# Hybrid decoder block on one core: a constant tile for the norm's eps, and where the pool of split operands begins

## The chip, the cores and the metric

The kernel runs on one core of one Trainium2 chip. The metric is the device time of one execution in microseconds (us). Before the change the median of three runs is 1487.4 us (1486.57 to 1491.19).

## What is computed

One decoder block for 1024 tokens of width 1024, float32 throughout. The reference, cut down:

```python
proj = x @ w_in                      # 1024 x 7168: q, f, i, og, pool_v, gate_a, gate_b
q = silu(q) * 128 ** -0.5;  f = lb + (1 - lb) * sigmoid(f);  k = 1 - f
o = hgrn2_chunked(q, k, i, log(f))   # 8 heads of 128: S_t = diag(f_t) S_{t-1} + k_t v_t^T, o_t = S_t^T q_t
o = o * rsqrt(mean(o ** 2, axis=-1) + RMS_EPS)          # the norm of the change, RMS_EPS = 1e-6
a = (o * hgrn_norm_g * sigmoid(og)) @ w_a
b = grouped(causal_mean(pool_v) - pool_v) @ w_pool * pool_scale
mix = (sigmoid(gate_a) * a + sigmoid(gate_b) * b) @ w_out
x = layer_norm(2 ** 0.25 * x + mix)
x = layer_norm(2 ** 0.25 * x + relu(x @ w_up) ** 2 @ w_down)
```

## The kernel before

**Products.** TensorE multiplies a stationary operand (up to 128 x 128) by a moving one (128 x up to 512) into PSUM. To keep float32's precision, each large product is made of three matmuls in the type fp32r: an operand is split into a high part (a cast on ScalarE) and a low part (a subtraction on VectorE), and high x high, high x low and low x high are added up in PSUM. Lines 108 to 110 (`mm3`), 202 to 205 (`prod`), 478 to 480 (`three`) and 1295 to 1297 (`down_tile`) are these three matmuls. In the profile a matmul is written with its moving operand first: `ps_pj<-act,w` moves an `act` tile past a stationary `w` tile. On top of that, the large products are Strassen products: seven instead of eight half-size ones (`p1` to `p7` in `pair`, line 264 on), with sums and differences of operands made on VectorE.

**Stages, in order of time.** First i = the value projection, by rows (`three`, to about 75 us). Then the eight heads, each in two halves of 512 tokens (`hgrn`, lines 819 to 946): the recurrence of a half is made of small plain float32 matmuls, many VectorE operations and a chain on GpSimd, while TensorE runs the projections of the next head, of the gates and of the pooling branch between them (`prod`, to about 600 us). Then the pool products (`pool_products`, line 709, by `mm3`), the product with w_a (`prod`), the product with w_out and the first layer norm (`mix`, `mm3`, from about 765 us), the up-projection (`prod`, to about 1160 us) and the down-projection (`down_tile`, to the end).

**Memory.** A core's on-chip memory is 128 partitions; a tile takes the same bytes in each, rounded up to 32. Pools on the left are laid one behind the other from byte 16512 on, pools on the right downward from the top. On the left stand, in this order, `const` (ident, cmask, eps_ln, inv_n, prm, lb, one_lb, e01), `stat` (eight tiles of 48 bytes allotted 64, four of 16 allotted 32), then `act`: 28 tiles of 4096 bytes, each the high and the low half of a split activation (later of anything that is split). Behind it stand `ca` (intermediate results) and, in turn, the heads' pool `hgp`, the rows of the first norm and the weights of the down-projection. On the right, under a pad of 24 floats (line 78), stand `wq` (the split weights `w`, raw weights, differences `t`) and, in turn, x, the heads' `q`, `f`, `og`, `v`, the split w_out rows `wo`, and buffers of the MLP. Which pool a tile is in is fixed in the code; the addresses follow from the sizes and the order.

**Order of the work.** A scheduler with a timeline of its own orders each engine's instructions, so the order can shift when an instruction's form changes.

**Lines the text speaks of.** 121 and 122: the split of a weight into `w`; 126 and 127: the split into `act`; 163: transposes; 242: a difference of raw weights; 595: loads. In `hgrn`: 824 the scan, 832 to 851 the small factors on GpSimd, 883 and 943 transposes, 888, 928, 931 the small products, 936 the squares and their sums (ScalarE), 940 the scaling by the root. Between 936 and 940 stands `inverse_root` (lines 795 to 805): on GpSimd, 4 numbers per partition, x = sum/128 + eps in line 798, a first guess from the bits (799), and three Newton steps of four operations (801 to 804), each waiting for the one before. 1305 loads rows with GpSimd's queue. `eps_ln` (lines 138 and 139) is the layer norms' own constant and is not changed.

Of the kernel before, what the change touches and what calls it, by code (L numbers as in the profile page):

```python
# [9 lines left out]
F32 = mybir.dt.float32  # L10
# [4 lines left out]
ALU = mybir.AluOpType  # L15

_TC = dict(schedule_with_timeline_sim=True)
P = 128
# [20 lines left out]
RMS_EPS = 1e-6  # L39
# [7 lines left out]
def tile_hybrid_block(  # L47
# [19 lines left out]
    V, A, G, PE = nc.vector, nc.scalar, nc.gpsimd, nc.tensor  # L67
# [5 lines left out]
    const = ctx.enter_context(tc.tile_pool(name="const", bufs=1))  # L73
# [51 lines left out]
    def split_into(t, src):  # L125
# [9 lines left out]
        out=cmask, in_=cmask, compare_op=ALU.is_ge, fill=0.0, base=0,  # L135
        pattern=[[1, P]], channel_multiplier=-1,
    )
    eps_ln = const.tile([P, 1], F32, name="eps_ln")
    G.memset(eps_ln, LN_EPS)
    inv_n = const.tile([P, HALO], F32, name="inv_n")  # L140
# [478 lines left out]
    with tc.tile_pool(name="tmp", bufs=1, side="right", reuse_waits="tile") as tmp:  # L619
# [18 lines left out]
        def small(tag, shape, bufs=2):  # L638
            n = math.prod(shape[1:])
            t = hgp.tile([P, max(n, LINE)], F32, tag=tag, name=nm(tag), bufs=bufs)[:, :n]  # L640
            return t if len(shape) == 2 else t.rearrange("p (a b) -> p a b", b=shape[2])
# [153 lines left out]
        def inverse_root(total):  # L795

            x, y, z = (small(tag, [P, CH]) for tag in ("rx", "ry", "rz"))
            G.tensor_scalar(x, total, 1.0 / P, RMS_EPS, ALU.mult, ALU.add)
            G.tensor_scalar(y.bitcast(I32), x.bitcast(I32), -0.5, ROOT_GUESS, ALU.mult, ALU.add)
            for _ in range(ROOT_STEPS):  # L800
                G.tensor_mul(z, y, y)
                G.tensor_mul(z, z, x)
                G.tensor_scalar(z, z, -0.5, 1.5, ALU.mult, ALU.add)
                G.tensor_mul(y, y, z)
            return y
# [13 lines left out]
        def hgrn(h, u, ft, q, v, og, state):  # L819
# [114 lines left out]
            for c in range(CH):  # L934
                w = slice(c * P, (c + 1) * P)
                A.activation(on[:, w], o[:, w], AF.Square, accum_out=ss[:, c : c + 1])
            ss = inverse_root(ss)
            for c in range(CH):
                w = slice(c * P, (c + 1) * P)
# [474 lines left out]
```

## Time and profile before

| | |
|---|---|
| median of the runs | 1487.4 us |
| the profiled execution | 1489.97 us |
| its span, first to last instruction | 1488.3 us |
| mean granted TensorE clock | 0.996 |
| TensorE matmul (PE) busy | 1463.3 us, 7377 instructions |
| VectorE (DVE) busy | 1142.0 us |
| ScalarE (ACT) busy | 714.3 us |
| GpSimd (POOL) busy | 119.9 us |
| `inverse_root` line 798 | 16 instructions, mean 326 ns |

The profile is of one execution. Its groups gather the instructions of one line, engine and operation: destination and sources by the program's names, shapes, count, busy time, the mean of one, and the idle time ahead of them with what ended it. Matmuls are pipelined and their ends modelled: what one costs in a row of many is the distance between starts, not its "mean". A view by windows gives each engine's busy time and number of instructions in stretches of the span. The text uses "phase" for a start address modulo 128 bytes.

### The profile page before, as it was taken

The numbers are of one execution on the slowest core, as the hardware profiler recorded it, in microseconds if no ns is written. First come the engines' busy times: TensorE is split into PE (matmuls) and PEld (weight loads), VectorE is DVE, ScalarE is ACT, GpSimd is POOL, SyncE is SP. The second block draws the span as 40 slices with busy tenths as digits, with TensorE's granted clock in tenths as the row PEclk, the third lists the DMA queues.
The fourth block names the chain that finished last, engine by engine and source line by source line (L and its number), as shares of the span: only waits on it lengthen the run. The fifth ranks groups of instructions, "written<-read, shape, count | busy, mean of one in ns | idle before, by whom it ended". The sixth has DMA issues, their size and how long they took to land.

```text
span 1488.3 us, 20830 instructions
## 1 busy us (share of the span) xinstructions
PE 1463.3 (98%) x7377; PEld 1191.6 (80%) x7377; DVE 1142.0 (77%) x1822; ACT 714.3 (48%) x1335; POOL 119.9 (8%) x467
## 2 busy tenths in 40 slices
PE   9999999999999998999999999999999999999997
PEld 7787888888888886777888878888888888888886
DVE  5957989899998775668985598666556797777978
ACT  5445455444455543456542366555555544343435
POOL 0001112111131121000002100000000100000000
PEclk9999999999999999999999999999999999999999
DMA  6232233323323456886663135444464774535422
GB/s 248 77 115 86 86 96 98 98 86 117 97 93 121 142 163 213 284 280 227 228 220 146 51 106 180 140 155 142 141 227 169 262 282 126 172 127 179 133 71 113
DMA packets 160616, 226.83 MB, mean 152 GB/s; under 512 B 11232, under 2 KB 84480, under 8 KB 160512
## 3 DMA queue, kind: packets, MB, share of 16 engines
q1 hardware_dynamic: 158576, 218.93, 44.2%
q0 software_dynamic: 1152, 4.19, 0.9%
q10 hardware_dynamic: 784, 2.38, 0.5%
q8 instruction: 58, 0.95, 0.3%
q14 instruction: 46, 0.38, 0.1%
HBM read 154.16 MB, written 71.30 MB: 151 GB/s over the span
## 4 chain that ended last, share of the span: by engine, by line
PE 94%; DMA 3%; DVE 2%; ACT 1%; issue 0%; SPq 0%; DVEq 0%; ACTq 0%
PE ps_pj L202 16%; PE ps_pj L205 16%; PE ps_pj L204 16%; PE ps_pj L1297 4%; PE ps_pj L1295 4%; PE ps_pj L1296 4%; PE ps_pj L109 2%; PE ps_pj L108 2%; PE ps_pj L110 2%; PE ps_tr L1297 1%; PE ps_tr L1295 1%; PE ps_tr L1296 1%; PE ps_sc L202 1%; PE ps_sc L205 1%; PE ps_sc L204 1%; PE ps_hg L202 1%
## 5 line engine op out<-in xcount | busy, mean ns | idle before, releaser
L202 PE MATMUL ps_pj<-act,w 128*128 128x512 f32 x1068 | 427.2, 400 | 2.3 <-DVE c L276 1.5
L204 PE MATMUL ps_pj<-act,w 128*128 128x512 f32 x1068 | 421.6, 396 | 0.5 <-DVE act L127 0.5
L205 PE MATMUL ps_pj<-act,w 128*128 128x512 f32 x1068 | 420.0, 397 | 0.0
L202 PEld LDWEIGHTS ps_pj<-act,w 128*128 128x128 f32 x1068 | 200.9, 188 | 50.8 <-DVE c L276 1.9
L205 PEld LDWEIGHTS ps_pj<-act,w 128*128 128x128 f32 x1068 | 200.9, 188 | 47.9
L204 PEld LDWEIGHTS ps_pj<-act,w 128*128 128x128 f32 x1068 | 200.9, 188 | 46.5 <-DVE act L127 0.9
L121 ACT CAST w<-t 128x512 fp32r<-128x512 f32 x170 | 104.9, 620 | 128.0 <-PE ps_pj L204 81.1
L121 ACT CAST w<-raw 128x512 fp32r<-128x512 f32 x143 | 88.3, 621 | 132.0 <-PE ps_pj L204 77.0
L122 DVE TENSOR_TENSOR w<-raw,w 128x512 fp32r<-128x512 f32 x143 | 100.2, 705 | 55.8 <-ACT w L121 54.0
L122 DVE TENSOR_TENSOR w<-t,w 128x512 fp32r<-128x512 f32 x170 | 116.4, 687 | 34.6 <-ACT w L121 33.5
L1257 ACT CAST act<-act 128x1024 fp32r<-128x1024 f32 x66 | 66.9, 1049 | 106.8 <-issue 35.0
L1296 PE MATMUL ps_pj<-act,act 128*128 128x512 f32 x240 | 93.0, 389 | 0.0
L1297 PE MATMUL ps_pj<-act,act 128*128 128x512 f32 x240 | 93.0, 389 | 0.0
L1258 DVE TENSOR_TENSOR act<-act,act 128x1024 fp32r<-128x1024 f32 x66 | 79.3, 1221 | 17.4 <-ACT act L1257 17.4
L1295 PE MATMUL ps_pj<-act,act 128*128 128x512 f32 x240 | 92.5, 389 | 0.0
L276 DVE TENSOR_TENSOR c<-c,ps_pj 128x512 f32<-128x512 f32 x95 | 64.7, 683 | 25.5 <-PE ps_pj L205 21.1
L272 ACT COPY c<-ps_pj 128x512 f32<-128x512 f32 x96 | 55.2, 582 | 20.9 <-PE ps_pj L205 17.8
L830 DVE RECIPROCAL tC<-tA 128x128 f32<-128x128 f32 x64 | 54.0, 907 | 0.0
L1296 PEld LDWEIGHTS ps_pj<-act,act 128*128 128x128 f32 x240 | 45.1, 188 | 9.4
L1297 PEld LDWEIGHTS ps_pj<-act,act 128*128 128x128 f32 x240 | 45.1, 188 | 9.3
L1295 PEld LDWEIGHTS ps_pj<-act,act 128*128 128x128 f32 x240 | 45.1, 188 | 9.3
L242 DVE TENSOR_TENSOR t<-raw,raw 128x512 f32<-128x512 f32 x43 | 29.7, 690 | 25.4 <-DMA raw<-in_w_in_dram 22.5
(414 smaller groups left out, 2748.5 us busy)
## 6 DMA issues: line engine op xcount, KB each, us to landing
h<-c SPq DMA_DIRECT2D x106, 256.0 KB, 2.2
act<-h SPq DMA_DIRECT2D x78, 256.0 KB, 3.0
raw<-in_w_in_dram SPq DMA_DIRECT2D x64, 256.0 KB, 3.4
draw<-in_w_down_dram SPq DMA_DIRECT2D x16, 1024.0 KB, 7.7
raw<-in_w_up_dram SPq DMA_DIRECT2D x30, 512.0 KB, 4.1
raw<-in_w_in_dram SPq DMA_DIRECT2D x18, 512.0 KB, 4.0
hf<-h SPq DMA_DIRECT2D x34, 256.0 KB, 3.0
c<-o SPq DMA_DIRECT2D x24, 256.0 KB, 3.7
```

The lines of the kernel that those rows point to most:

```text
L121: A.copy(hi, src)
L122: V.tensor_sub(lo, src, f(hi))
L202: PE.matmul(ps, wh[:, k], th, start=first and k == 0, stop=False, skip_group_check=True)
L204: PE.matmul(ps, wh[:, k], tl, start=False, stop=False, skip_group_check=True)
L205: PE.matmul(ps, wl[:, k], th, start=False, stop=k == CH - 1, skip_group_check=True)
L272: A.copy(t, ps)
L276: V.tensor_add(t, t, ps)
L1257: A.copy(hi, src)
L1258: V.tensor_sub(lo, src, f(hi))
L1295: PE.matmul(ps, hh[:, w], wh, start=fresh and n == 0, stop=False, skip_group_check=True)
L1296: PE.matmul(ps, hh[:, w], wl, start=False, stop=False, skip_group_check=True)
L1297: PE.matmul(ps, hl[:, w], wh, start=False, stop=n == M - 1, skip_group_check=True)
```

## The change

A new tile of one float per partition is filled with RMS_EPS among the constants, and line 798 (now 800) reads its second scalar from it in place of a number in the instruction:

```diff
@@ -135,6 +135,8 @@
         out=cmask, in_=cmask, compare_op=ALU.is_ge, fill=0.0, base=0,
         pattern=[[1, P]], channel_multiplier=-1,
     )
+    eps_rms = const.tile([P, 1], F32, name="eps_rms")
+    G.memset(eps_rms, RMS_EPS)
     eps_ln = const.tile([P, 1], F32, name="eps_ln")
     G.memset(eps_ln, LN_EPS)
     inv_n = const.tile([P, HALO], F32, name="inv_n")
@@ -795,7 +797,7 @@
         def inverse_root(total):
 
             x, y, z = (small(tag, [P, CH]) for tag in ("rx", "ry", "rz"))
-            G.tensor_scalar(x, total, 1.0 / P, RMS_EPS, ALU.mult, ALU.add)
+            G.tensor_scalar(x, total, 1.0 / P, eps_rms, ALU.mult, ALU.add)
             G.tensor_scalar(y.bitcast(I32), x.bitcast(I32), -0.5, ROOT_GUESS, ALU.mult, ALU.add)
             for _ in range(ROOT_STEPS):
                 G.tensor_mul(z, y, y)
```

The tile is allotted 32 bytes ahead of eps_ln, so all that stands behind it on the left moves up by 32 bytes, `act` among it. Lines behind the insertion are numbered two higher in the changed kernel.

## The prediction

> **What bounds the kernel now.** I read the page first: the span, the busy shares, the chain that ended last.
>
> ```profile
> span 1488.3 us, 20830 instructions
> PE 1463.3 (98%) x7377; PEld 1191.6 (80%) x7377; DVE 1142.0 (77%) x1822; ACT 714.3 (48%) x1335; POOL 119.9 (8%) x467
> PE 94%; DMA 3%; DVE 2%; ACT 1%; issue 0%; SPq 0%; DVEq 0%; ACTq 0%
> ```
>
> TensorE is busy 98% and holds 94% of the chain, so the span is the number of matmuls times the spacing of their starts, plus a few gaps. That spacing is the quantity to look at, and the groups hide it: their "mean ns of one" is a modelled latency of about 390 ns, of which consecutive matmuls overlap. So I counted matmuls in two long windows where TensorE has nothing else to run: the up-projection, then the down-projection (columns: PE busy and count, granted clock, DMA).
>
> ```profile
> 930.00:1150.00 220.00, 220.00 (x944) 1.00 0.48 165
> 1200.00:1440.00 240.00, 240.00 (x1060) 1.00 0.48 157
> ```
>
> A window counts every matmul that touches it, so one latency is added to its length: (220 + 0.4)/944 = 233.5 ns, and (240 + 0.4)/1060 = 226.8 ns. All are 128x512 products of split operands at full clock. The first kind takes **6.7 ns** more.
>
> What differs? In the up-projection the moving operand is an `act` tile and the stationary one a `w` tile; in the down-projection both are `act` tiles. The out-projection mixes the kinds within a few microseconds, at one line group, with `act` stationary throughout. The first two rows below are the first and last of 66 consecutive matmuls, the next three a later stretch, the last two the first and last of 24 in the pool products.
>
> ```profile
> 770.19 0.39 PE L108 MATMUL ps_pj<-act,act 128*128 128x512 f32 x1
> 784.92 0.39 PE L110 MATMUL ps_pj<-act,act 128*128 128x512 f32 x1
> ...
> 785.15 0.40 PE L108 MATMUL ps_pj<-w,act 128*128 128x512 f32 x1
> 786.55 0.39 PE L108 MATMUL ps_pj<-act,act 128*128 128x512 f32 x1
> ...
> 787.93 0.40 PE L108 MATMUL ps_pj<-wo,act 128*128 128x512 f32 x1
> 789.34 0.40 PE L108 MATMUL ps_pj<-wo,act 128*128 128x512 f32 x1
> ...
> 658.51 0.39 PE L108 MATMUL ps_pj<-w,q 128*128 128x512 f32 x1
> 663.72 0.39 PE L110 MATMUL ps_pj<-w,f 128*128 128x512 f32 x1
> ```
>
> `act,act`: (784.92 - 770.19)/65 = 226.6 ns. `w,act`: six in 1.40 us, 233.3 ns. `wo,act`: six in 1.41 us, 235 ns. `w` with `q` or `f`: (663.72 - 658.51)/23 = 226.5 ns. So neither `act` nor `w` is slow in itself; only some pairings are. Nor is it the load on the other engines: the kinds change within one chain of 24 products.
>
> The allotment fits this. Bytes per partition, each tile rounded up to 32: the constants begin at 16512 and take 512 + 512 (ident, cmask), 32 (eps_ln), 64 (inv_n), 128 (prm), 32 + 32 + 64 (lb, one_lb, e01), then stat 8 x 64 + 4 x 32. So `act` begins at 16512 + 2016 = 18528 = 144 x 128 + 96: phase 96 modulo 128, and as an act tile is 4096 bytes, every half of every one. The right-hand pools (`w`, `wo`, `q`, `f`, `og`, `v`) stand at phase 0 in the built program. Fast pairings have equal phases (96 with 96, 0 with 0), slow ones unequal.
>
> **The change part by part.** *The new tile.* eps_rms is four bytes, allotted 32, so everything behind it in the left pools moves up by 32 and `act` begins at 18560 = 145 x 128, phase 0. The right-hand pools stay. Every split operand is then at phase 0. These are the matmuls that have unequal phases now (one row each for lines 202, 204, 205 and 478 over the whole span, PE busy and count, then PEld; and the two unequal kinds of line 108):
>
> ```profile
> 0.00:1488.30 1488.30, 491.94 (x1232) 231.76 (x1232) 1.00 0.46 152
> 0.00:1488.30 1488.30, 485.85 (x1232) 231.76 (x1232) 1.00 0.46 152
> 0.00:1488.30 1488.30, 484.14 (x1232) 231.69 (x1232) 1.00 0.46 152
> 0.00:1488.30 1488.30, 41.91 (x112) 21.03 (x112) 1.00 0.46 152
> ...
> L108 PE MATMUL ps_pj<-wo,act 128*128 128x512 f32 x32 | 12.7, 397 | 0.0
> L108 PE MATMUL ps_pj<-w,act 128*128 128x512 f32 x16 | 6.3, 396 | 0.0
> ```
>
> 3 x 1232 + 3 x 112 + 3 x (32 + 16) = 4176 (lines 479 and 480 have as many as 478, and 109 and 110 as 108). At 6.7 ns each: **28.0 us**. The down-projection gains nothing, since its pairs are equal already.
>
> The trace has one row that does not show the effect:
>
> ```profile
> L163 PE MATMUL ps_tr<-ident,x 128*128 128x128 f32 x56 | 7.6, 273 | 0.0
> L163 PE MATMUL ps_tr<-ident,r 128*128 128x128 f32 x56 | 8.3, 272 | 0.0
> ```
>
> ident and x have equal phases (0, 0), ident and r unequal ones (0, 96), and the transposes take the same. They are plain float32 of 128 columns; I take the effect to belong to the 512-column products only, and give the small ones nothing.
>
> *What a faster TensorE runs into.* Engine busy times by stage (PE, PEld, DVE, ACT, POOL, clock, DMA), and under them line 202 alone (PE, PEld) in the heads' two windows and from 560 to 680:
>
> ```profile
> 75.00:295.00 220.00, 220.00 (x1313) 178.47 (x1312) 179.42 (x332) 107.78 (x243) 38.50 (x164) 1.00 0.31 96
> 295.00:515.00 220.00, 220.00 (x1448) 180.74 (x1447) 197.85 (x387) 109.70 (x267) 42.82 (x186) 1.00 0.35 112
> 560.00:600.00 40.00, 31.32 (x203) 25.12 (x202) 20.34 (x39) 15.27 (x45) 4.68 (x20) 0.95 0.67 211
> 600.00:680.00 80.00, 77.67 (x326) 61.44 (x325) 54.17 (x85) 39.57 (x73) 1.60 (x9) 0.98 0.86 286
> 700.00:745.00 45.00, 45.00 (x195) 36.27 (x194) 42.68 (x71) 23.70 (x42) 0.00 (x0) 1.00 0.73 246
> 855.00:893.00 38.00, 36.85 (x174) 29.33 (x173) 35.68 (x60) 22.97 (x43) 0.00 (x0) 1.00 0.35 109
> ...
> 75.00:295.00 220.00, 98.63 (x245) 46.13 (x245) 1.00 0.31 96
> 295.00:515.00 220.00, 105.68 (x262) 49.34 (x262) 1.00 0.35 112
> 560.00:680.00 120.00, 41.71 (x105) 19.56 (x104) 0.97 0.80 261
> ```
>
> From 560 to 680 TensorE already idles 11 us behind the last head's chain, and the DMA engines are 86% busy after it. It has 3 x 105 long products of unequal phase, worth 2.1 us; I count all of that as lost. From 700 to 745 the gain would be 195 x 6.7 = 1.3 us where DVE has 2.3 us free, and from 855 to 893 1.2 us where it has 2.3 us free and TensorE already waits; I count half of each as lost, 1.2 us. In the heads (75 to 515) DVE is 82 and 90% busy; 3 x 507 long products are worth 10.2 us of 440, which leaves DVE at 88% on average (377 us of 430), and I count that as gained. Together 3.3 us lost.
>
> *The operand of eps.* Line 798 reads its second scalar from a tile, 16 times. POOL's chain behind it is waited for once in full view:
>
> ```profile
> 583.90 0.40 PE L205 MATMUL ps_pj<-act,w 128*128 128x512 f32 x1
> 587.10 0.33 PE L943 MATMUL ps_tr<-ident,tH 128*128 128x128 f32 x1 [2.79 <-ACT tH L940]
> ...
> L802 POOL TENSOR_TENSOR rz<-rz,rx 128x4 f32<-128x4 f32 x48 | 14.1, 295 | 2.9
> L803 POOL TENSOR_SCALAR rz<-rz 128x4 f32<-128x4 f32 x48 | 13.0, 270 | 3.5
> L832 POOL COPY T<-tA 128x32 f32<-128x32 f32 x16 | 6.7, 416 | 89.2 <-DVE tA L824 88.8
> ```
>
> No instruction of this form is in the trace. Nearest rows: a second SBUF operand costs 295 against 270 ns, 25 ns; from above, the dearest small operation, 416, 146 ns; from below, the same 25 ns saved. Times 16: -0.4 to 2.3 us, if no cover stood over any. In all heads but the last, TensorE runs the next head's products meanwhile; queued behind it on POOL are only the other lines of the same root and the factors of the next half head. I take 25 ns each, 0.3 us. The added memset and its neighbours lie ahead of the first product, under 0.1 us each.
>
> *The shift for the other engines and DMAs.* The same 512 elements take DVE as long at phase 0 as at 96, and a load of 256 KB lands as soon in `act` (96) as in `hf` (0):
>
> ```profile
> L122 DVE TENSOR_TENSOR w<-t,w 128x512 fp32r<-128x512 f32 x170 | 116.4, 687 | 34.6 <-ACT w L121 33.5 <-PE ps_pj L479 1.2
> L127 DVE TENSOR_TENSOR act<-ps_tr,act 128x512 fp32r<-128x512 f32 x22 | 14.7, 687 | 15.8 <-ACT act L126 15.5
> ...
> act<-h SPq DMA_DIRECT2D x78, 256.0 KB, 3.0
> hf<-h SPq DMA_DIRECT2D x34, 256.0 KB, 3.0
> ```
>
> So nothing there. The order of instructions is the same on DVE, ACT and SP; on PE two transposes swap places twice, on POOL steps of two roots interleave otherwise in a few heads. I count these as nothing, under the products that surround them; uncovered, a swap is one transpose of 0.27 us.
>
> *Sum.* 28.0 - 3.3 - 0.3 = 24.4 us. The profiled execution took 1489.97 us around its span of 1488.3; it would come to 1465.6, its span to 1463.9. The median of the runs shown is 1487.4, 2.6 below that execution, so the forecast is **1463 us**.
>
> **The rivals.**
>
> *Distance, not phase: no change.* Phase and place are confounded here. All act pairs lie in the lower half of the partition (18528 to 133216) and all fast pairs at phase 0 in the upper (171648 to 220800), while every slow pair joins the two. If the distance between operands makes the 6.7 ns, nothing moves but line 798: 1487.4 + 0.3, so 1488. For it speaks that no pair separates the two readings; against it that within the halves pairs 100 KB apart are as fast as neighbours. The Trainium skill has a rule with the same result: "TensorE: Matmul & The Clock Gate", section "Step-by-step: what each phase is for", says that PE has two independent SBUF read ports, so that a weight load takes no read bandwidth from the running matmul. By it no start address of an operand would matter, and the time would stay; the spread of 226.6 to 235 ns within one chain disagrees.
>
> *The gain is eaten.* If DVE cannot follow in the heads, those 10.2 us are lost too: 24.4 - 10.2 = 14 us, 1473. For it, DVE's 90% from 295 to 515; against it, TensorE shows no idle time in either window.
>
> *The clash turns around: slower.* Equal phases in opposite halves is a pairing that no long product has now. If equal phases collide there, as unequal ones seem to now, the same 4176 products pay once more: 28 us, 1515. It decides from the first product on, wherever line 202 starts more than 233.5 ns apart. Against it, ident (low) with x (high), both at phase 0, is no slower than with r.
>
> **How the numbers follow.** Forecast 0.72 (1457 to 1470), eaten 0.10, no change 0.12, slower 0.06. Without losses, and with the half-clock stretch near 600 us (clock 0.95) gone too, it is 1457; the eaten case with 2 us more lost gives 1475. 1457 to 1475 holds the first two cases, 0.8. A measurement of this kernel tells about 0.3% from no change: faster 0.82, same 0.12, slower 0.06.
>
> **What would show it.** In the changed profile the window of the up-projection should hold matmuls 226 to 227 ns apart, and the `act,w` groups should show a mean near 390 instead of 396 to 400, with lines 1295 to 1297 unchanged. If `act,w` stays at 396, distance was the cause. If it falls and the time falls less than 20 us, idle time ahead of PE has grown, first between 560 and 745 us. Line 798's mean shows the price of the operand. I am wrong altogether if line 202 gets slower.

## The result, and the profile after

| | before | changed |
|---|---|---|
| median | 1487.66 us (1486.57 to 1491.19) | 1467.5 us (1465.99 to 1468.02) |
| profiled execution | 1489.97 us, span 1488.3 | 1468.02 us, span 1466.3 |

The medians are of four executions each; the 1487.4 us given ahead of the prediction is that of the first three. The ratio is 0.9859, with a 95% interval of 0.9841 to 0.9877: faster by 20 us between the medians, by 22.0 us between the two profiled spans. The forecast was 1463, the range 1457 to 1475. One execution of all those in this document, one of the ten of e10 below, took 2069.83 us at a mean granted clock of 0.653 and does not enter its ratio.

The page of the changed kernel: span, busy times (share of the span, instructions) and the costliest groups of matmuls (count | busy us, mean ns of one | idle us ahead of them). The two added lines move 202, 204, 205 and 1295 to 204, 206, 207 and 1297.

```profile
span 1466.3 us, 20831 instructions
...
PE 1440.2 (98%) x7377; PEld 1192.6 (81%) x7377; DVE 1139.4 (78%) x1822; ACT 713.9 (49%) x1335; POOL 126.6 (9%) x468
...
L204 PE MATMUL ps_pj<-act,w 128*128 128x512 f32 x1068 | 420.7, 394 | 2.7 <-DVE c L278 2.2
L206 PE MATMUL ps_pj<-act,w 128*128 128x512 f32 x1068 | 414.9, 390 | 0.5 <-DVE act L127 0.5
L207 PE MATMUL ps_pj<-act,w 128*128 128x512 f32 x1068 | 413.4, 390 | 0.6 <-DVE w L122 0.6
...
L1297 PE MATMUL ps_pj<-act,act 128*128 128x512 f32 x240 | 92.4, 389 | 0.0
```

The same groups of the kernel before, and one of the down-projection:

```profile
L202 PE MATMUL ps_pj<-act,w 128*128 128x512 f32 x1068 | 427.2, 400 | 2.3 <-DVE c L276 1.5 <-ACT og L272 0.3 <-DVE q L730 0.2
L204 PE MATMUL ps_pj<-act,w 128*128 128x512 f32 x1068 | 421.6, 396 | 0.5 <-DVE act L127 0.5
L205 PE MATMUL ps_pj<-act,w 128*128 128x512 f32 x1068 | 420.0, 397 | 0.0
...
L1295 PE MATMUL ps_pj<-act,act 128*128 128x512 f32 x240 | 92.5, 389 | 0.0
```

TensorE runs the same 7377 matmuls and is still busy 98%. PE's busy time has shrunk by 1463.3 - 1440.2 = 23.1 us, so the gain lies inside its busy time and not in idle time removed. The `act,w` groups fell from 396 to 400 ns to 390 to 394; the `act,act` group stays at 389.

The means are latencies; the price is the distance between starts. The windows of the changed kernel, PE alone, at the places used before:

```profile
930.00:1150.00 220.00, 220.00 (x973) 1.00 0.50 172
1200.00:1440.00 240.00, 240.00 (x1060) 1.00 0.40 132
```

(220 + 0.4)/973 is 226.5 ns in the up-projection, where it was 233.5; the down-projection holds the same 1060 matmuls as before, 226.8 ns. The two kinds of product now cost the same. The out-projection says it product by product. The timeline of the changed kernel (start us, duration, engine, line), the first of each six:

```profile
773.02 0.39 PE L108 MATMUL ps_pj<-w,act 128*128 128x512 f32 x1
...
774.38 0.39 PE L108 MATMUL ps_pj<-act,act 128*128 128x512 f32 x1
...
775.74 0.39 PE L108 MATMUL ps_pj<-wo,act 128*128 128x512 f32 x1
...
777.10 0.39 PE L108 MATMUL ps_pj<-wo,act 128*128 128x512 f32 x1
```

Each six takes 1.36 us, 226.7 ns a product, whichever pool the moving operand comes from; the same sixes with `w` or `wo` took 1.40 and 1.41.

**Where the gain arose.** The start of the same matmul (the k-th on PE) in both traces gives the time gained up to it. The expected column is 6.7 ns for each long product that had unequal phases:

| stretch of before, us | such products | at 6.7 ns, us | gained, us |
|---|---|---|---|
| 0 to 75 | 250 | 1.7 | 0.8 |
| 75 to 560, the heads | 1771 | 11.9 | 8.3 |
| 560 to 680 | 310 | 2.1 | 0.6 |
| 680 to 765 | 340 | 2.3 | 2.3 |
| 765 to 893 | 300 | 2.0 | 1.9 |
| 893 to 1190 | 1205 | 8.1 | 8.0 |
| behind 1190 | 0 | 0 | 0 |

From 680 us on the gain is the full price. What is missing is missing ahead of that, most of it in the heads. The table compares one execution with one. A second trace of the changed kernel (e8 below) gives the heads 8.2 us as well, but the stretch from 560 to 680 us 2.7 in place of 0.6; and in e5, where the `act,w` products still pay in full, that stretch is 2.7 us shorter than before too. So the 0.6 us say little about the products there.

### The profile page after: what moved, and what is told of

Same layout as the page of the kernel before. It is cut to its first block, busy times and chain, and to the rows that moved or that the text cites. A ratio compares the mean times of both kernels' runs of the same rounds, so it can differ in the third digit from the quotient of the medians.

```text
span 1466.3 us, 20831 instructions
## 1 busy us (share of the span) xinstructions
PE 1440.2 (98%) x7377; PEld 1192.6 (81%) x7377; DVE 1139.4 (78%) x1822; ACT 713.9 (49%) x1335; POOL 126.6 (9%) x468
## 4 chain that ended last, share of the span: by engine, by line
PE 57%; DVE 2%; DMA 2%; ACT 1%; issue 0%; SPq 0%; POOL 0%; DVEq 0%; ACTq 0%
PE ps_pj L204 7%; PE ps_pj L206 7%; PE ps_pj L207 7%; PE ps_pj L1297 4%; PE ps_pj L1299 4%; PE ps_pj L1298 4%; PE ps_pj L109 2%; PE ps_pj L110 2%; PE ps_pj L108 2%; PE ps_tr L1297 1%; PE ps_tr L1299 1%; PE ps_tr L1298 1%; PE ps_sc L204 1%; PE ps_sc L206 1%; PE ps_sc L207 1%; PE ps_hg L206 1%
## 5 line engine op out<-in xcount | busy, mean ns | idle before, releaser
L204 PE MATMUL ps_pj<-act,w 128*128 128x512 f32 x1068 | 420.7, 394 | 2.7 <-DVE c L278 2.2
L206 PE MATMUL ps_pj<-act,w 128*128 128x512 f32 x1068 | 414.9, 390 | 0.5 <-DVE act L127 0.5
L207 PE MATMUL ps_pj<-act,w 128*128 128x512 f32 x1068 | 413.4, 390 | 0.6 <-DVE w L122 0.6
```

Source lines behind the costliest of these rows:

```text
L204: PE.matmul(ps, wh[:, k], th, start=first and k == 0, stop=False, skip_group_check=True)
L206: PE.matmul(ps, wh[:, k], tl, start=False, stop=False, skip_group_check=True)
L207: PE.matmul(ps, wl[:, k], th, start=False, stop=k == CH - 1, skip_group_check=True)
```

## The experiments

In the built program of the kernel before, `w`, `wo`, `q` and `f` begin at 128 modulo 256 and `act` at 18528, which is 96 modulo 256; the slices taken of both lie at multiples of 512 bytes. *Distance* below is the start of `act` less that of the weight tile, modulo 256: -32 before, 0 in the changed kernel. A tile added to the constants moves `act` and leaves the weights where they are. The theory of the prediction is that operands of equal phase modulo 128 are cheap; the first rivals are that the absolute alignment does it, or the edit to the operand. To compare all of them, one window of the up-projection, 930 to 1130 us, serves for every run; before, then the changed kernel:

```profile
930.00:1130.00 200.00, 200.00 (x858) 1.00 0.49 170
```

```profile
930.00:1130.00 200.00, 200.00 (x884) 1.00 0.49 170
```

200.4/858 = 233.6 ns and 200.4/884 = 226.7 ns. Some 858 matmuls in this window mean the full price, 884 none.

**e1_shift_only**: the kernel before with an unused tile of 32 bytes in the place of `eps_rms`; the operand stays immediate.

```diff
+    G.memset(const.tile([P, 8], F32, name="shift"), 0.0)
     eps_ln = const.tile([P, 1], F32, name="eps_ln")
```

> The left pools moved up by 32 bytes by an unused tile; line 798 keeps its immediate eps. Theory A (equal start phases modulo 128 bytes of the moving and the stationary operand make the 128x512 split products 227 ns apart, unequal ones 233 ns): all the gain, act,w groups at about 390 ns, 1464 to 1468 us; if the tile operand of line 800 and the half clock after it cost 2 us or more, this run is up to 3 us below the changed kernel. Rival O (the tile operand, by another order on GpSimd, brings the gain): 1487 us, act,w at 396 to 400 ns.

1467.3 us (1464.86 to 1468.07), ratio 0.9855 (0.9842 to 0.9868). The window of this kernel:

```profile
930.00:1130.00 200.00, 200.00 (x884) 1.00 0.49 170
```

The shift alone gives the whole gain; what the tile holds and who reads it makes no difference that these intervals show.

**e2_operand_only**: the changed kernel with 96 bytes more ahead of `eps_ln`, so that `act` stands at 224 modulo 256, distance +96.

```diff
     G.memset(eps_rms, RMS_EPS)
+    G.memset(const.tile([P, 24], F32, name="shift"), 0.0)
```

> Line 798 reads eps from the tile, but three more unused tiles follow, so that the left pools move up by 128 bytes in all and act stays at phase 96. Theory A: no gain, 1487 to 1490 us (the operand alone, 0 to 2 us), act,w at 396 to 400 ns. Rival O: 1465 to 1470 us.

1490.11 us (1488.43 to 1491.72), ratio 1.001 (1.0001 to 1.0019).

```profile
930.00:1130.00 200.00, 200.00 (x859) 1.00 0.49 169
```

With the operand and without the equal start nothing is gained; the interval leaves 0.1 to 2.8 us for the operand and the new distance together.

**e3_all_at_96**: the kernel before, with the right-hand pools moved down by 32 bytes instead of `act` up: all split operands at 96.

```diff
-    G.memset(pad.tile([P, 24], F32, name="pad_top"), 0.0)
+    G.memset(pad.tile([P, 32], F32, name="pad_top"), 0.0)
```

> Nothing on the left is moved; the pad at the top of the right pools grows from 96 to 128 bytes, so that w, wo, q, f and the others on the right stand at phase 96 like act. Theory A, equal phases whatever they are: the same gain, 1464 to 1469 us, act,w at 390 ns. Rival B, each operand must itself start on a multiple of 128: no gain or a loss, 1487 us or more, act,w at 396 ns or more.

1467.41 us (1466.92 to 1472.46), ratio 0.9866 (0.9852 to 0.9881).

```profile
930.00:1130.00 200.00, 200.00 (x884) 1.00 0.49 171
```

No long operand begins on a multiple of 128 bytes here, and the gain is all there. At equal starts, 96 serves as well as 0 modulo 128: what counts is where the two operands lie relative to each other.

**e4_apart_64**: the kernel before with 96 bytes ahead of `eps_ln`: distance +64.

```diff
+    G.memset(const.tile([P, 24], F32, name="shift"), 0.0)
     eps_ln = const.tile([P, 1], F32, name="eps_ln")
```

> The left pools moved up by 96 bytes, so that act stands at phase 64 and the right pools at 0. If the period of theory A is 128 bytes: no gain, 1485 to 1490 us, act,w near 396 ns. If the period is 64 bytes or less: the gain, 1464 to 1469 us, act,w near 390 ns. A value between would mean that the price depends on the distance of the phases.

1476.0 us (1475.39 to 1477.48), ratio 0.9917 (0.9902 to 0.9932). The window, then groups of the same kernel by shape:

```profile
930.00:1130.00 200.00, 200.00 (x876) 1.00 0.49 169
```

```profile
L203 PE MATMUL ps_pj<-act,w 128*128 128x512 f32 x1068 | 422.2, 396 | 1.4 <-DVE c L277 1.2 <-ACT act L126 0.2
L205 PE MATMUL ps_pj<-act,w 128*128 128x512 f32 x1068 | 417.4, 392 | 0.5 <-DVE act L127 0.5
...
L480 PE MATMUL ps_pj<-w,act 128*128 128x512 f32 x64 | 25.3, 396 | 0.0
```

200.4/876 = 228.8 ns: a third of the price. The groups show a direction. Line 205, where `act` moves and lies 64 ahead of the weights, has 392 ns; line 480, where `w` moves and lies 64 behind, has 396 as before. By the distances of starts the first takes about 229 ns, the second 233.3.

**e5_apart_32** and **e6_shift_160**: two more sizes of the same tile, 64 and 160 bytes: distance +32, and +128, which is equal modulo 128.

```diff
+    G.memset(const.tile([P, 16], F32, name="shift"), 0.0)   # e5
+    G.memset(const.tile([P, 40], F32, name="shift"), 0.0)   # e6
```

> The left pools moved up by 64 bytes: act at phase 32, the right pools at 0. Theory A: no gain in the direction that 64 apart still paid in full (moving w or wo past act). For moving act past w the runs so far give 233.3 ns at 96 and 229.3 ns at 64. If the price depends only on how many bytes the moving operand is ahead, modulo 128, 32 is a new value: full price 1485 to 1490 us, half price near 1476, none 1465 to 1469. I expect full price, as 32 and 96 are mirror images.

> The left pools moved up by 160 bytes: act at phase 0 modulo 128 again, but 128 bytes apart from w modulo 256. If the period is 128: the whole gain, 1464 to 1469 us. If it is 256 or 512: a pitch over 228 ns for act,w and 1472 us or more.

e5: 1488.27 us (1487.38 to 1489.99), ratio 0.9996 (0.9987 to 1.0005). e6: 1486.13 us (1484.63 to 1487.51), ratio 0.9981 (0.9972 to 0.9991). Their windows, e5 first:

```profile
930.00:1130.00 200.00, 200.00 (x859) 1.00 0.48 166
```

```profile
930.00:1130.00 200.00, 200.00 (x859) 1.00 0.48 166
```

e5 pays in full, so 32 bytes ahead cost as much as 32 behind. e6 breaks the rule of the prediction: its phases modulo 128 are equal, and each product costs 233.3 ns (the ratio leaves it at most 0.3% faster than before).

**e9_shift_288**: the next candidate, a period of 256 bytes against one of 512: distance 256.

```diff
+    G.memset(const.tile([P, 72], F32, name="shift"), 0.0)
```

> The left pools moved up by 288 bytes: act is 256 bytes apart from w modulo 512 (0 in the changed kernel, 128 in the run with 160 bytes, which kept the full price). If the period is 256 bytes: the whole gain, 1464 to 1469 us, act,w near 390 ns. If it is 512 bytes (the length of one row of the 128-column stationary operand): a price again, 1475 to 1488 us.

1466.62 us (1464.82 to 1468.71), ratio 0.985 (0.9831 to 0.9869).

```profile
930.00:1130.00 200.00, 200.00 (x884) 1.00 0.49 170
```

256 is as free as 0. So a period of 256 bytes fits all runs; only at this one distance was a repeat tried.

**e7_idle_products** and **e8_changed_again**: the stretch behind the last heads. In the changed kernel it gained 0.6 us where 2.1 would have been possible, and the granted clock from 560 to 600 us is 0.83 where it was 0.95. e7 puts 18 products that nobody uses into the wait for the root of the last head; the rest of the computation is unchanged. e8 is the changed kernel once more, on the same chip.

```diff
+        root_x = []
+
         def inverse_root(total):
             x, y, z = (small(tag, [P, CH]) for tag in ("rx", "ry", "rz"))
+            root_x.append(x)
...
             pt = ps_tile("tr", 2)
+            for _ in range(18 if (h, u) == (HEADS - 1, 0) else 0):
+                PE.matmul(pt[:CH, :P], root_x[-1], ident, start=True, stop=True)
```

> The changed kernel with 18 products of no use (4 stationary columns, 128 moving ones), which wait for the first step of the root of head 7, first half, and so fill TensorE's longest wait of 4.4 us. The clock was half for 13.7 us after it. Theory H, the wait of TensorE brings the half clock and it costs up to 6 us: the half-clock stretches shrink to 7 us or less and the time falls by 2 to 5 us. Rival: the chain on GpSimd, ScalarE and VectorE sets this stage whatever the clock: no change or up to 1 us slower.

> The changed kernel itself on this chip, for the pairs above: 1466 to 1469 us.

e7: 1465.09 us (1464.4 to 1467.03), ratio 0.9842 (0.9826 to 0.9858). e8: 1465.43 us (1463.92 to 1467.16), ratio 0.9843 (0.9826 to 0.9859). Windows of e7, then of e8 (PE busy, granted clock):

```profile
570.00:600.00 30.00, 26.12 (x145) 0.94 0.61 201
```

```profile
570.00:600.00 30.00, 21.36 (x95) 0.83 0.58 192
```

The products raise the granted clock from 0.83 to 0.94, and the time stays the same within its spread. The 2 to 5 us that were expected if the lower clock set the end of this stretch are not there; a microsecond could not be told apart with four executions each.

**e10_low_parts_moved**, **e11_low_alone_apart**, **e12_rings_control**: how local is the price? The changed kernel, with the high and the low parts of the weights in two rings of their own and a small tile between them. Each sum step runs high, high, low weights (lines 204, 206, 207). In e10 the high parts are 32 bytes off and the low parts equal; in e11 the low parts alone are 32 off; in e12 both are equal, as a control for the rings.

```diff
-        return wq.tile([P, CH, P], F32R, tag="w", name=nm("w"), bufs=NW)
+        n_w[0] += 1
+        if n_w[0] == 2:
+            G.memset(wq.tile([P, 8], F32, name="gap"), 0.0)    # e12: 64
+        tag = "w" if n_w[0] % 2 else "wl"
+        t = wq.tile([P, CH, P], F32R, tag=tag, name=nm(tag), bufs=NW // 2)
+        if n_w[0] == 2:                                        # e11 only
+            G.memset(wq.tile([P, 56], F32, name="gap2"), 0.0)
+        return t
```

> The changed kernel with high and low parts of a weight in two rings, 32 bytes between them: low parts equal with act, high parts 32 bytes apart from it. In the order high x high (204), high x low (206), low x high (207), theory N (a matmul is slowed by the weights that are loaded beside it, those of the next matmul) expects 204 and 207 slow at 233 ns and 206 fast at 227 ns; theory W (by its own weights) expects 204 and 206 slow, 207 fast. Either way two thirds of the gain of line 204 to 207 go: 1478 to 1484 us.

> Two rings again, but now the high parts of the weights are a multiple of 256 bytes apart from act (no price so far) and the low parts alone 32 bytes off. Theory S (one unequal weight load in three keeps the whole stream slow, as in the run before): no gain beyond a few us, 1484 to 1490 us, lines 204 to 207 at 394 to 402 ns. Theory N or W (each matmul pays for one load): two thirds of the gain stay, 1471 to 1476 us, and one of the three lines alone is slow.

> The control for the two rings: the gap between them is 256 bytes, so that high and low parts are both a multiple of 256 bytes apart from act. If the period is 256 and the rings cost nothing: the time of the changed kernel, 1464 to 1470 us. If the rings themselves (two of five in place of one of ten) cost the time: 1480 us or more.

e10: 1491.6 us, ratio 1.0013 (1.0003 to 1.0022). e11: 1489.97 us (1487.34 to 1493.71), ratio 1.0005 (0.9994 to 1.0016). e12: 1472.09 us (1471.2 to 1474.23), ratio 0.9883 (0.9868 to 0.9898). Their windows in this order:

```profile
930.00:1130.00 200.00, 200.00 (x859) 1.00 0.50 171
```

```profile
930.00:1130.00 200.00, 200.00 (x859) 1.00 0.49 170
```

```profile
930.00:1130.00 200.00, 200.00 (x884) 1.00 0.49 169
```

The control has 226.7 ns, so the two rings cost nothing in spacing; they cost about 5 us elsewhere, since the ratio is 0.9883 and not 0.985. A price for each product by itself would make two products in three slow in e10 and one in three in e11, and so would a price by the load that runs under each product: about 693 and 687 ns for three, against 680 in the changed kernel. Both kernels pay in full instead. The groups of e10, then of e11, show how the price is spread:

```profile
L204 PE MATMUL ps_pj<-act,w 128*128 128x512 f32 x1068 | 428.4, 402 | 3.7 <-ACT c L280 1.5 <-ACT w L121 1.1 <-DVE c L284 1.0
L206 PE MATMUL ps_pj<-act,w 128*128 128x512 f32 x1068 | 422.4, 397 | 0.0
L207 PE MATMUL ps_pj<-act,wl 128*128 128x512 f32 x1068 | 418.3, 394 | 0.0
```

```profile
L204 PE MATMUL ps_pj<-act,w 128*128 128x512 f32 x1068 | 427.1, 400 | 4.3 <-ACT w L121 1.1 <-DVE c L287 1.1 <-ACT act L126 1.0
L206 PE MATMUL ps_pj<-act,w 128*128 128x512 f32 x1068 | 425.7, 400 | 0.0
L207 PE MATMUL ps_pj<-act,wl 128*128 128x512 f32 x1068 | 415.1, 391 | 0.0
```

The distances from the starts of lines 204, 206 and 207 to the next, over the whole span, are 235.0, 233.1 and 231.0 ns in e10 and 232.1, 238.0 and 228.9 ns in e11. The single product moves by up to 5 ns, but the sum of three is 699 ns in both, 3 x 233.0. One unequal operand in three keeps the whole stream at the slow pace. The trace of before fits this: the six equal `act,act` products between two unequal sixes, 786.55 to 787.93 us in the lines of the prediction, took 1.38 us, 230 ns each and not 226.6, so a slow product still weighs on the next few. Why that is so stays open; no run here looks inside TensorE.

**All distances on one line each.** Spacing in the up-projection by the same window:

| distance modulo 256, from the moving operand | kernel | spacing, ns | ratio of times |
|---|---|---|---|
| 0 | changed, e1, e3, e9 | 226.7 | 0.985 to 0.987 |
| -32 | before | 233.6 | 1 |
| +32 | e5 | 233.3 | 0.9996 |
| +64 | e4 | 228.8 | 0.9917 |
| +96 | e2 | 233.3 | 1.001 |
| 128 | e6 | 233.3 | 0.9981 |

-64 and -96 were seen only in products of the out-projection with `w` or `wo` moving, by the distances of their starts: 233.3 ns in e4 and 233.5 ns in e2.

## Why the prediction was right, and where not

**What bounds the kernel, and the price of a product: right.** 6.7 ns for each long `act,w` product, found by counting matmuls in windows, came back as 6.9 (233.6 to 226.7). The order of the instructions on PE and POOL, which the change moves, cost nothing that shows: e1, without the operand, has the ratio of the changed kernel.

**The rule behind it: the step that failed.** The prediction held that operands of equal phase modulo 128 are cheap. e6 has equal phases modulo 128 and pays in full; e9 shows the period of 256. The forecast came out because a shift of 32 bytes closes the distance under either rule, and that was luck: with the weights 128 bytes elsewhere, the same rule and the same sum would have forecast the same 24.4 us, and e6 shows that nearly nothing would have come. In the trace of before the two couldn't be told apart: all its fast long pairs lay at distances equal modulo 256 as well. The reading "begins on a multiple of 128 bytes" isn't the cause either (e3).

**Distance, not phase: wrong as it was meant,** as the distance between far parts of the memory; a distance does count, but modulo 256 bytes. The lower and the upper half of the partition are joined by the same products now at 226.7 ns. The sentence of the Trainium skill that was weighed there ("TensorE: Matmul & The Clock Gate", "Step-by-step: what each phase is for": two read ports independent of each other) would leave the spacing alone whatever the start; the runs disagree, with 226.7 against 233 ns by the distance of the starts alone. That the ports collide is not shown by this.

**The clash turns around: wrong**, by the first window of the changed kernel.

**The sum: 24.4 us forecast, 22.0 measured between the profiled spans.** Four terms were mis-sized:

- *The heads, counted as gained in full.* 75 to 560 us gained 8.3 of 11.9, so 3.6 us are missing. The reason was not the rival's, a busy VectorE. Windows of the changed kernel (PE, PEld, DVE, ACT, POOL, clock, DMA):

```profile
75.00:295.00 220.00, 218.84 (x1328) 180.90 (x1328) 181.18 (x338) 107.39 (x243) 40.28 (x164) 1.00 0.31 98
295.00:515.00 220.00, 220.00 (x1471) 184.13 (x1470) 197.18 (x386) 113.58 (x272) 46.01 (x186) 1.00 0.36 113
```

  VectorE is as busy as before (181.18 and 197.18 against 179.42 and 197.85), and TensorE stays busy over the whole second window. The first has 1.2 us of idle time that was not there before. The rest is spacing: behind six or more long products in a row it fell from 233.28 to 226.97 ns, 6.3 ns; with a small float32 product among the six before, only from 232.7 to 230.6, 2.1 ns (distances under 300 ns), over some 320 products. Against 6.7 that is 320 x 4.6 = 1.5 us and 1451 x 0.4 = 0.6 us; with the idle time 3.3 of the 3.6 us. Behind small products in between, the long ones do not come down to the full pace.

- *The first 75 us* gained 0.8 of 1.7, which the prediction didn't list apart. Why stays open.

- *560 to 680 us, counted as nothing,* gave 0.6 of 2.1 in this pair of traces, 2.7 with e8's; *the edges at 700 to 745 and 855 to 893, half of it counted as lost,* lost 0.1 us and not 1.2. That VectorE's 2.3 us of free time there were enough fits, but was not tried by itself.

- *The operand, 25 ns each, at most 146.* The groups by shape on POOL, of the kernel before, the changed one, and e1:

```profile
L798 POOL TENSOR_SCALAR rx<-ss 128x4 f32<-128x4 f32 x16 | 5.2, 326 | 176.1 <-ACT tH L936 175.7
```

```profile
L800 POOL TENSOR_SCALAR rx<-ss,eps_rms 128x4 f32<-128x4 f32 x16 | 9.1, 569 | 167.9 <-ACT tH L938 167.8
```

```profile
L799 POOL TENSOR_SCALAR rx<-ss 128x4 f32<-128x4 f32 x16 | 4.9, 304 | 169.5 <-ACT tH L937 169.2
```

  The mean is 243 ns more than before, ten times the term and above its upper end: 3.9 us of POOL's time over 16. But the means mix two cases. The same step of the last head's first half, with no VectorE instruction beside it, in the kernel before and in the changed one:

```profile
582.82 0.19 POOL L798 TENSOR_SCALAR rx<-ss 128x4 f32<-128x4 f32 x1 [23.30 <-ACT tH L936]
```

```profile
573.40 0.27 POOL L800 TENSOR_SCALAR rx<-ss,eps_rms 128x4 f32<-128x4 f32 x1 [23.67 <-ACT tH L938]
```

  So the operand alone costs 0.08 us, three times the term and inside its bounds. Eight of the sixteen took 0.26 or 0.27 us, where nine took 0.19 before; the others, all beside VectorE instructions, took 0.48 to 1.85 us, where seven took 0.43 to 0.69. Most of the 243 ns is this longer wait, which the prediction had no term for. The cover that the prediction named, TensorE on the next head's products, stood over nearly all of it: e1, without the operand, and the changed kernel have ratios of 0.9855 and 0.9859.

Together: the heads and the first 75 us lost 4.5 us more than counted, 560 to 680 and the two edges 1.7 less, and the operand's 0.3 is inside these stretches: 24.4 - 4.5 + 1.7 + 0.3 = 21.9.

**The stretch behind the last head** deserves its own look, since idle time grew there as the prediction's last part had feared. The timeline of the changed kernel, the last round of one root (POOL), the sums of the heads' outputs (DVE, in `o_sums`) beside it, and the transposes that wait for it:

```profile
576.28 0.20 POOL L803 TENSOR_TENSOR rz<-ry 128x4 f32<-128x4 f32 x1
576.53 0.69 DVE L611 TENSOR_TENSOR c<-c,c 128x512 f32<-128x512 f32 x1 [3.93 <-DMA c<-o]
576.56 0.73 POOL L804 TENSOR_TENSOR rz<-rz,rx 128x4 f32<-128x4 f32 x1
...
577.37 0.63 POOL L805 TENSOR_SCALAR rz<-rz 128x4 f32<-128x4 f32 x1
577.99 0.69 DVE L613 TENSOR_TENSOR c<-c,c 128x512 f32<-128x512 f32 x1
578.09 0.65 POOL L806 TENSOR_TENSOR ry<-ry,rz 128x4 f32<-128x4 f32 x1
...
579.19 0.47 PE L945 MATMUL ps_tr<-ident,tH 128*128 128x128 f32 x1 [4.39 <-ACT tH L942]
```

A step of the root takes 0.20 us alone and 0.63 to 0.73 beside a VectorE addition of two operands in SBUF. TensorE waits 4.39 us for the end of this chain, where it waited 2.79 before. TensorE reached this place 9 us earlier, and other VectorE work fell beside the root. How much differs between executions: in e8, the same kernel, one step alone was slowed (0.62 us) and TensorE waited 3.39 us. The chain on POOL and ScalarE ends this wait, which fits that e7's higher clock on TensorE brought no gain that shows.

## What to carry to other kernels

When equal-looking long matmuls have two spacings in the trace, count them in windows, sort them by the tiles of both operands, and compare the start addresses of moving and stationary operand: here a difference that is a multiple of 256 bytes saved 6.7 ns of 233, and any one operand out of line kept the stream slow. A pool's start is set by whatever small tile was allotted ahead of it, so a change of a few bytes in a constants pool can be worth more than the edit it belongs to; test the shift and the edit apart. And a rule that fits the traces at hand (modulo 128) needs a run at a point where its neighbours (modulo 256, absolute alignment) say otherwise.

## What the runs showed of the hardware that was not expected

- The start address of the stationary operand relative to the moving one sets the pace of 128x512 products of split operands: 226.7 ns at 0 modulo 256, 233 ns at 32 and at 96 to either side and at 128, 228.8 ns at +64 but 233.3 at -64.
- It is a pace of the stream: one unequal weight load in three costs as much as three (699 ns for three products in e10 and e11 alike), and with a small float32 product among the six before, the long ones take 230.6 ns even at equal starts.
- A scalar operand read from a tile made a 128x4 `tensor_scalar` on POOL take 0.27 us in place of 0.19 with no VectorE instruction beside it; the mean of 16 rose from 326 to 569 ns, since beside VectorE instructions it took up to 1.85 us.
- POOL's 128x4 steps took 0.63 to 0.73 us beside VectorE additions with both inputs in SBUF, and 0.20 us alone. The Trainium skill states that a VectorE instruction with two inputs in SBUF contends with a GpSimd instruction that reads SBUF ("SBUF — State Buffer", "Who interferes with whom"); this trace agrees.
